# Modulation vectors by VectorE sums, an empty GpSimd, and due times in the planner of a two-layer diffusion backbone

## The chip, the cores and the metric

One core of a Trainium2 chip. The metric is the device time of one execution in microseconds, taken as the median of three runs. Engines are named as in the profile: PE (TensorE), DVE (VectorE), ACT (ScalarE), POOL (GpSimd), SP (SyncE, which issues the loads). PSUM is the memory that TensorE writes its products to, SBUF the other on-chip memory.

## The reference

Two layers work on 256 latent and 256 context tokens of 1024 features. Each has a SwiGLU FFN half step, a mixer, and a second FFN half step, all with a modulated RMS norm ahead:

```python
for l in range(DEPTH):
    mod_lat = jnp.split((silu_c @ w_mod[l] + b_mod[l])[:, None, :], N_MOD, axis=-1)
    mod_ctx = jnp.split((silu_cc @ w_mod[l] + b_mod[l])[None, None, :], N_MOD, axis=-1)
    x = macaron_half(x, mod_lat[0:3], norm_ffn1[l], w_ffn1_in[l], w_ffn1_out[l])
    ctx = macaron_half(ctx, mod_ctx[0:3], norm_ffn1[l], w_ffn1_in[l], w_ffn1_out[l])
    h_lat = modulate(rms_norm(x, norm_mix[l]), mod_lat[3], mod_lat[4])
    ...
    y_lat, y_ctx = hybrid_mixer(h_lat, h_ctx, w_in[l], ...)
    x = x + mod_lat[5] * (y_lat @ w_out[l])
    x = macaron_half(x, mod_lat[6:9], norm_ffn2[l], w_ffn2_in[l], w_ffn2_out[l])
    ...
return x
```

`macaron_half` is x + 0.5 * gate * swiglu(rms_norm(x) * (1 + scale) + shift); the FFN has 2816 hidden features. So each layer needs nine modulation vectors of 1024 features, for the latent condition c and for the context condition c_ctx, from a matrix w_mod of 1024 x 9216. The mixer runs two groups of heads on one input projection: eight heads of neighbourhood attention, and four heads of a DeltaNet in both directions. The DeltaNet's q, k and v pass a short convolution of five taps and a Silu, q and k are normalised and, for latent tokens, rotated (rope); chunks of 64 tokens need the inverse of I + A, with A the masked, decayed Gram matrix of the keys; the scans over the chunks carry a state. Both groups share an output projection. In layer 1 only the latent stream is finished.

## The kernel before

**Numbers and tiles.** Activations lie with features on partitions. Every dense product is split exactly into high and low parts in a rounded format (fp32r) and takes three products on TensorE (`mm3`). SP loads each weight tile of 128 x 1024 float32 (512 KB) into one of four buffers `wr`, ScalarE rounds it to `wh`, VectorE subtracts to `wl`. In the profile the products of an FFN read s (normed input) or d and n (hidden values), and wh or wl.

**Order.** The kernel isn't emitted as it is written. `Recorder` takes down every instruction with its data dependences; `plan` makes list schedules of all of them (`Schedule`) from a table of costs (`cost_of`) and the buffers that are free, at three widths of look-ahead, three times over, each in the order that the last one found; `emit` writes the best of them out, with products of zeros (`keep_warm`) where TensorE would idle. So all instructions have one line in the profile, L661 (L653 for the zeros, L680 and L672 after the change), and are told apart by the names of their tiles. An engine's next instruction is the ready one of lowest rank in the order before. All engines then run their own fixed queues.

**Modulation.** The first norm's two vectors come from `mods_first` by TensorE, from 32 half-size loads (n<-w_mod). The 16 others (`mods`; seven in the first FFN, four in the second FFN of layer 0, five in the first FFN of layer 1; twelve for two conditions, four for one) are sums on VectorE: the eight row tiles of w_mod's columns are scaled by the condition's value on each partition and added up, in pieces of 512 (or 1024) columns, in tiles `m`. `ps<-m,con` are the products with ones that add over the partitions; ScalarE copies the result, VectorE transposes it and adds the bias.

**The norm.** `norm_stats` and `norm_spread` make 1/rms of the tokens and spread it over partitions. `norm_apply` makes the normed, modulated input: for even feature tiles two VectorE operations (d<-x,na,d and s<-d,md,s) and one of ScalarE, for odd ones a GpSimd product (d<-x,d), two ScalarE operations and one of VectorE (s<-d,s). The running sums of squares are GpSimd's (`square_sum`).

**The DeltaNet.** `dn_qkv` makes q, k, v of a head from eight products in PSUM; ScalarE copies the sum (raw) and VectorE adds the four outer taps of the convolution (n<-n,sm,n of 508 and 510 elements, and half of that). `dn_prep` normalises (d<-ps,t) and, on GpSimd, rotates. `gate_math` is a chain of operations of 32 elements (gp, gs) on VectorE. `dn_unit` makes A for a token tile from decays and the keys' Gram matrix: its factors rg (n<-con,gh on VectorE and n<-con,gl on GpSimd) and B (d<-con,ex, d<-d,d, GpSimd). `dn_base` inverts blocks of 32, `dn_merge` merges them to 128; masks of the merge (wr<-d,con) are GpSimd's.

The GpSimd branch of the norm, as an example:

```python
nc.gpsimd.tensor_tensor(h, self.x[d][:, c], bs[:, :TL], O.mult)
nc.scalar.activation(h, h, self.A.Identity, bias=sh, scale=a[:, d, s:s + 1])
nc.scalar.copy(hh, h)
nc.vector.tensor_tensor(hl, h, hh.bitcast(F32), O.subtract)
```

Of the kernel before, what the change touches and what calls it, by code (L numbers as in the profile page):

```python
# [101 lines left out]
def lay_out(a):  # L102
# [11 lines left out]
        "xt": np.ascontiguousarray(xt.reshape(KD, 128, T).transpose(1, 0, 2)),  # L114
        "cc": np.stack([feat(a["c"][0]), feat(a["c_ctx"])], axis=-1),
# [19 lines left out]
class View:  # L135
    """A part of a planned tile: the cells it covers and how to reach it from the tile."""
# [39 lines left out]
def regroup(a, pat, kw):  # L176
    """numpy's view of an axis rearrangement in the notation of access patterns."""
# [31 lines left out]
class Sym:  # L209
    """A tile of the plan: a class of equal slots, and the slot that it is given."""  # L210
# [18 lines left out]
class Recorder:  # L229
    """Takes down the instructions of the kernel with their data dependences."""  # L230
# [9 lines left out]
    def tile(self, cls, bufs, shape, dtype, make, dram=False):  # L240
        """a new tile: the whole of it as a view."""
# [36 lines left out]
    def add(self, eng, ops):  # L278
# [3 lines left out]
        n.cost = sum(self.cost(eng, *o) for o in ops)  # L282
        n.columns = sum(columns_of(*o) for o in ops) if eng == "tensor" else 0
# [66 lines left out]

TABLES = {"Silu": "silu", "Exp": "exp", "Sqrt": "sqrt"}


class Pool:
    """A tile pool of the plan."""
# [26 lines left out]
class Clock:  # L382
    """The tensor engine's clock: half of its rate after a tick that counted few columns."""
# [6 lines left out]
    def run(self, t, cost, columns):  # L390
        """when work of so much time at the full rate and so many columns ends that begins at t."""
# [11 lines left out]
class Schedule:  # L403
    """Times for all nodes: a list schedule on the engines with the tiles' slots as a further resource."""

    def __init__(self, rec, rank, window, shift=None):
        self.rec, self.rank, self.window = rec, rank, window
        self.prio = [r - n.ahead for r, n in zip(rank, rec.nodes)]
        if shift:
            self.prio = [p + s for p, s in zip(self.prio, shift)]  # L410
# [3 lines left out]
    def prepare(self):  # L414
        """program order of the tiles in each class and how many are live where one begins."""
# [23 lines left out]
    def run(self):  # L439
# [22 lines left out]
        busy = {e: 0.0 for e in engs}  # L462
        table = None
# [12 lines left out]
        def foresee(i, at):  # L476
            """when urgent work can begin that is about to have all it waits for."""
# [7 lines left out]
        def claim(n):  # L485
            """slots for the tiles that begin with n, or the class that has none."""
# [43 lines left out]
        while done < len(nodes):  # L530
            # advance
# [19 lines left out]
            while again:  # L551
              again = False
              for e in engs:
                  held = []
                  while avail[e] and busy[e] <= t + 1e-9:
# [29 lines left out]
                      if e == "tensor":  # L585
# [3 lines left out]
                          en = clock.run(st, cost, n.columns)  # L589
                      else:  # L590
# [34 lines left out]
def keep_warm(rec, sched, cls):  # L625
    """matmuls of zeros into free PSUM slots where the tensor engine would stand idle."""
# [36 lines left out]

def plan(rec):
    """the best of a few schedules, each in the order that the one before it found."""
    n = len(rec.nodes)
    rank, best = list(range(n)), None
    for _ in range(3):
        found = min((Schedule(rec, rank, w).run() for w in (4, 12, 20)), key=lambda s: s.time)
        if best is None or found.time < best.time:  # L670
            best = found
        rank = [0] * n  # L672
        for k, i in enumerate(sorted(range(n), key=lambda i: (found.start[i], i))):
            rank[i] = k
    return best


def columns_of(name, a, kw):
# [3 lines left out]
    v = a[2]  # L682
# [1250 lines left out]
```

## Time and profile before

| | |
|---|---|
| median of three runs | 2002.95 us (2002.57 to 2003.49) |
| the profiled execution's own time | 2003.49 us |
| its span in the profile | 2003.5 us |
| stretches: start, first FFN | 0 to 42, 42 to 408 us |
| mixer of layer 0: units, merges | 450 to 550, 620 to 650 us |
| second FFN of layer 0, first of layer 1 | 776 to 1130, 1153 to 1515 us |
| mixer of layer 1: units, merges | 1560 to 1640, 1700 to 1730 us |
| second FFN of layer 1 | 1810 to 2004 us |

[...] Rows of operations give the tiles as out<-in, the count, the busy time and the mean of one in ns.

### The profile page before, as it was taken

The page shows a single profiled execution, that of the slowest core. Times are in us where ns is not written, and L with a number is a line of the kernel's source. Part 1 is how long each engine was busy: PE and PEld are TensorE (multiplying, and loading weights), DVE is VectorE, ACT ScalarE, POOL GpSimd, SP SyncE. Part 2 cuts the span into 40 slices and gives each one's busy share as a digit, 9 for nine tenths or more (in the row PEclk, how much of TensorE's full clock was granted, in tenths as well). Part 3 has the DMA queues.
Part 4 walks back from the last instruction along what each step waited for, and adds up shares of the span by engine and source line. Part 5 has one row for each costly group of instructions (what it writes and reads, how often), then busy time and mean ns, then how long its engine had stood idle before and what let it go on. Part 6 is the DMA issues. An engine that isn't in the chain of part 4 may idle for free.

```text
span 2003.5 us, 29224 instructions
## 1 busy us (share of the span) xinstructions
PE 1935.0 (97%) x11164; PEld 1621.5 (81%) x11164; DVE 1413.9 (71%) x2606; ACT 802.6 (40%) x1507; POOL 254.0 (13%) x257
## 2 busy tenths in 40 slices
PE   8999999998999999999999999999999789899999
PEld 5777777896787889777788888788888667699999
DVE  5777778879986979877333786553347999886555
ACT  4323222264546455332222433222126554755433
POOL 2000000036413003000000200000003641210000
PEclk8999999999998999999999999999999899899999
DMA  8556555541223223655233257653334133245653
GB/s 305 180 182 195 172 176 179 180 152 60 64 63 95 96 64 107 218 190 179 84 105 95 75 190 241 188 180 95 95 96 158 58 89 85 80 132 156 182 179 126
DMA packets 103611, 277.82 MB, mean 139 GB/s; under 512 B 26928, under 2 KB 30384, under 8 KB 103472
## 3 DMA queue, kind: packets, MB, share of 16 engines
q1 hardware_dynamic: 103472, 275.97, 43.9%
q8 instruction: 87, 1.43, 0.3%
q14 instruction: 52, 0.43, 0.1%
HBM read 267.54 MB, written 8.39 MB: 138 GB/s over the span
## 4 chain that ended last, share of the span: by engine, by line
PE 78%; DVE 16%; ACT 2%; issue 2%; DMA 1%; POOL 0%; SPq 0%; DVEq 0%; ACTq 0%; POOLq 0%
PE ps L661 78%; DVE n L661 3%; DVE d L661 3%; DVE t L661 2%; DVE wl L661 2%; DVE s L661 2%; DVE wh L661 1%; DVE x L661 1%; DVE gp L661 1%; DVE m L661 1%; ACT d L661 0%; ACT n L661 0%; ACT wh L661 0%; SPq L661 0%; ACT s L661 0%
## 5 line engine op out<-in xcount | busy, mean ns | idle before, releaser
L661 PE MATMUL ps<-s,wh 128*128 128x512 f32 (+2 forms) x3344 | 923.3, 364 | 6.6 <-ACT s L661 4.1
L661 PEld LDWEIGHTS ps<-s,wh 128*128 128x128 f32 (+1 forms) x3344 | 593.1, 190 | 116.4 <-issue 9.4
L661 PE MATMUL ps<-s,wl 128*128 128x512 f32 (+1 forms) x1672 | 606.1, 363 | 2.8 <-DVE wl L661 2.8
L661 ACT CAST wh<-wr 128x1024 fp32r<-128x1024 f32 (+2 forms) x341 | 350.0, 1037 | 612.5 <-PE ps L661 296.1
L661 DVE TENSOR_TENSOR wl<-wr,wh 128x1024 fp32r<-128x1024 f32 (+2 forms) x341 | 412.1, 1219 | 155.0 <-ACT wh L661 151.7
L661 PEld LDWEIGHTS ps<-s,wl 128*128 128x128 f32 x1672 | 317.3, 190 | 53.6 <-DVE wl L661 3.2
L661 PE MATMUL ps<-d,wh 128*128 128x256 f32 (+1 forms) x1344 | 297.5, 317 | 0.1
L661 DVE SCALAR_TENSOR_TENSOR m<-wr,sc,m 128x512 f32<-128x512 f32 (+1 forms) x364 | 267.2, 792 | 30.2 <-DMA wr<-w_mod 30.1
L661 PEld LDWEIGHTS ps<-d,wh 128*128 128x128 f32 x1344 | 220.3, 189 | 22.8 <-issue 3.0
L661 POOL TENSOR_TENSOR d<-d,d 128x256 f32<-128x256 f32 (+1 forms) x69 | 63.2, 916 | 1306.5 <-ACT d L661 1303.0
L661 DVE SCALAR_TENSOR_TENSOR x<-ps,hg,x 128x256 f32<-128x256 f32 x224 | 95.0, 477 | 174.4 <-PE ps L661 174.4
L661 PE MATMUL ps<-d,wl 128*128 128x256 f32 (+1 forms) x672 | 211.3, 314 | 0.0
L661 PE MATMUL ps<-n,wh 128*128 128x512 f32 (+1 forms) x640 | 179.2, 366 | 0.0
L661 PE MATMUL ps<-wh,s 128*128 128x512 f32 (+1 forms) x544 | 157.6, 364 | 0.2 <-ACT d L661 0.2
L661 ACT ACTIVATE d<-ps 128x512 f32<-128x512 f32 (+2 forms) x108 | 56.7, 530 | 209.2 <-PE ps L661 207.4
L661 DVE TENSOR_TENSOR d<-d,ps 128x512 f32<-128x512 f32 (+1 forms) x88 | 54.4, 619 | 113.5 <-PE ps L661 92.8
L661 PEld LDWEIGHTS ps<-d,wl 128*128 128x128 f32 x672 | 126.8, 189 | 8.5
L661 PEld LDWEIGHTS ps<-n,wh 128*128 128x128 f32 x640 | 114.8, 189 | 23.1 <-ACT wh L661 1.7
L661 PE MATMUL ps<-n,wl 128*128 128x512 f32 (+2 forms) x416 | 130.2, 347 | 0.0
L661 PEld LDWEIGHTS ps<-wh,s 128*128 128x128 f32 x544 | 97.3, 189 | 21.2 <-issue 5.6
L661 PE MATMUL ps<-wl,s 128*128 128x512 f32 (+1 forms) x272 | 97.6, 359 | 3.3 <-DVE wl L661 3.1
L661 DVE TENSOR_TENSOR d<-d,d 128x512 fp32r<-128x512 f32 (+29 forms) x248 | 83.6, 369 | 10.9 <-ACT d L661 6.8
(167 smaller groups left out, 1855.2 us busy)
## 6 DMA issues: line engine op xcount, KB each, us to landing
wr<-w_in SPq DMA_DIRECT2D x171, 512.0 KB, 4.1
wr<-w_mod SPq DMA_DIRECT2D x128, 512.0 KB, 3.7
wr<-w_out SPq DMA_DIRECT2D x104, 512.0 KB, 4.1
wr<-wd SPq DMA_DIRECT2D x24, 512.0 KB, 3.7
n<-w_mod SPq DMA_DIRECT2D x32, 256.0 KB, 5.4
wr<-wg SPq DMA_DIRECT2D x8, 528.0 KB, 3.5
xd<-x SPq DMA_DIRECT2D x16, 256.0 KB, 2.2
x<-xd SPq DMA_DIRECT2D x16, 256.0 KB, 2.7
```

What stands on the lines that cost most here:

```text
L661: getattr(eng, name)(*[rv(x) for x in a], **{q: rv(x) for q, x in k.items()})
```

## The change

**Modulation.** w_mod is packed with the 1024 rows of an output feature along the free dimension. `cond_rows` loads c and c_ctx, spread over all partitions, into two `m` tiles (512 KB each; three times in the program), and ScalarE takes their Silu. `mods` then makes one multiply-and-sum (`tensor_tensor_reduce`) for each tile of 128 output features and condition, which starts from the bias and leaves its sum in `md`; in the order it is two instructions of VectorE, printed ISA (junk and md, then md alone: the read of the accumulator). 224 such pairs take the place of 416 operations on VectorE, 64 products, 16 transposes, 16 additions and 16 ScalarE copies.

**GpSimd.** The norm's odd tiles go as the even ones, `bs` may stay in PSUM, sums of squares are VectorE's. Rope is VectorE's, from PSUM, and ScalarE scales by the norm afterwards, a tile at a time. rg's low part and B are scaled copies of ScalarE, four for each tile. The merge's masks are VectorE's, and a mask on A goes, as the last merge product is cut into halves (64 products of 64 x 64 instead of 32). The convolution reads PSUM without a copy. GpSimd has 36 instructions left of 262.

**Planner.** `due_times` gives every instruction the latest time by which it has to be done for TensorE's order; engines beside TensorE take the ready instruction that is due first. [...] Seven rounds instead of three, slightly other costs for products, 22 `d` buffers instead of 23.

```diff
 def pack_mod(w):
-    v = w.reshape(L, KD, 128, 9, 8, 4, 32)
-    return np.ascontiguousarray(v.transpose(0, 3, 1, 2, 5, 4, 6)).reshape(L, 9, KD, 128, 1024)
+    return np.ascontiguousarray(w.reshape(L, D, 9, KD, 128).transpose(0, 2, 3, 4, 1))
...
+        if due:
+            self.prio = [d if n.eng != "tensor" else p for p, d, n in zip(self.prio, due, rec.nodes)]
...
+                      elif n.port:
+                          en = port = max(st, port) + cost
...
+def due_times(rec, rank):
+    nodes, t, at = rec.nodes, 0.0, {}
+    for n in sorted((n for n in nodes if n.eng == "tensor"), key=lambda n: rank[n.i]):
+        t += n.cost
+        at[n.i] = t
+    due = [t + 50.0] * len(nodes)
+    for n in reversed(nodes):
+        due[n.i] = min([at.get(n.i, due[n.i])] + [due[j] - nodes[j].cost - LAT[n.eng][nodes[j].eng] for j in n.succs])
+    return due
...
-    for _ in range(3):
-        found = min((Schedule(rec, rank, w).run() for w in (4, 12, 20)), key=lambda s: s.time)
+    for _ in range(7):
+        found = min((Schedule(rec, rank, w, due).run() for w in (4, 12, 20)), key=lambda s: s.time)
...
+    def cond_rows(self):
+        nc = self.nc
+        self.cb = []
+        for n in range(2):
+            row = self.wp.tile([128, 1024], self.F32, name=self.nm("cb"), tag="m", bufs=self.BUFS["m"])
+            nc.sync.dma_start(row, self.io["cr"][:, n].to_broadcast([128, D]))
+            nc.scalar.activation(row, row, self.A.Silu)
+            self.cb.append(row)
+        yield
...
     def mods(self, l, lc, m, ns=2):
...
+        nc, O, md, cb = self.nc, self.O, lc["md"], self.cb
+        for d in range(KD):
             raw = self.wide("wr", "wr")
...
+            nc.sync.dma_start(raw[:, :D], self.io["w_mod"][l, m, d])
+            for n in range(ns):
+                c = 8 * m + d
+                nc.vector.tensor_tensor_reduce(self.junk, raw[:, :D], cb[n], 1.0, lc["bmod"][:, c:c + 1], O.mult, O.add, accum_out=md[:, c, n:n + 1])
+            yield
...
-            raw, acc = self.slot("cr", "n"), self.slot("ca", "n")
-            nc.scalar.copy(raw[:, :tok], ps[:, :tok])
+            acc = self.slot("ca", "n")
...
-            rv = raw[:, :tok].rearrange("p (s t) -> p s t", s=ns)
+            rv = ps[:, :tok].rearrange("p (s t) -> p s t", s=ns)
...
         for b in range(2):
-            nc.gpsimd.tensor_tensor(tv[:, :, b], ov[:, :, 1 - b], sn[:, :, b], O.mult)
-        nc.gpsimd.tensor_tensor(out[:, :TL], out[:, :TL], self.rope[:, 0], O.mult)
-        nc.gpsimd.tensor_tensor(out[:, :TL], out[:, :TL], tmp[:, :TL], O.add)
+            nc.vector.tensor_tensor(tv[:, :, b], pv[:, :, 1 - b], sn[:, :, b], O.mult)
+        nc.vector.tensor_tensor(out[:, :TL], ps[:, :TL], self.rope[:, 0], O.mult)
+        nc.vector.tensor_tensor(out[:, :TL], out[:, :TL], tmp, O.add)
+        for t, c in enumerate(tiles):
+            nc.scalar.activation(out[:, c], out[:, c] if t < 2 else ps[:, c], A.Copy, scale=rs[:, t:t + 1])
...
+            rg.append((d, self.slot("rg", "n", self.F32R)))
+            for h in range(4):
+                nc.scalar.activation(rg[-1][1][:, hc(h)], m, A.Copy, scale=self.gl.bitcast(F32)[:, t, 4 * d + h:4 * d + h + 1])
...
-            nc.gpsimd.tensor_tensor(self.h3(b), m3((self.lt, self.gt)[d]), b3(self.beta[:, t, 4 * d:4 * d + 4]), O.mult)
-        nc.gpsimd.tensor_tensor(B, B, B1, O.add)
+            for h in range(4):
+                nc.scalar.activation(b[:, hc(h)], (self.lt, self.gt)[d], A.Copy, scale=self.beta[:, t, 4 * d + h:4 * d + h + 1])
+        nc.vector.tensor_tensor(B, B, B1, O.add)
```

On VectorE in the first FFN, the sums of a vector (m, two conditions) stood between the low weight halves (wl) like this before:

```order
L661 SCALAR_TENSOR_TENSOR m_801<-wr_920,sc_81,m_801 128x2x256 x2
L661 SCALAR_TENSOR_TENSOR m_793<-wr_940,sc_81,m_793 128x2x256 x2
L661 SCALAR_TENSOR_TENSOR m_801<-wr_940,sc_81,m_801 128x2x256 x2
L661 TENSOR_TENSOR wl_1013<-wr_957,wh_984 128x1024
L661 TENSOR_TENSOR wl_1023<-wr_969,wh_996 128x1024
L661 SCALAR_TENSOR_TENSOR m_793<-wr_994,sc_81,m_793 128x2x256
L661 TENSOR_TENSOR d_1030<-d_1030,ps_953 128x512
L661 SCALAR_TENSOR_TENSOR m_793<-wr_994,sc_81,m_793 128x2x256
L661 SCALAR_TENSOR_TENSOR m_801<-wr_994,sc_81,m_801 128x2x256
L661 TENSOR_TENSOR n_1054<-d_1030,n_1045 128x512
```

and now, with md the vectors, junk a result that nothing reads, and m the two rows of conditions:

```order
L680 TENSOR_TENSOR wl_923<-wr_820,wh_916 128x1024
L680 ISA junk_803,md_400<-wr_884,m_657,sm_370 128x1024
L680 ISA md_400 128x1
L680 TENSOR_TENSOR d_948<-d_948,ps_874 128x512
L680 TENSOR_TENSOR wl_963<-wr_862,wh_955 128x1024
L680 TENSOR_TENSOR n_971<-d_948,n_961 128x512
L680 ISA junk_803,md_400<-wr_940,m_638,sm_370 128x1024
L680 ISA md_400 128x1
L680 ISA junk_803,md_400<-wr_940,m_657,sm_370 128x1024
L680 ISA md_400 128x1
L680 TENSOR_TENSOR wl_999<-wr_898,wh_994 128x1024
```

Two ISA pairs take the place of four operations of 512 elements, and the low halves stand between them as before.

On SP at the start, loads of the first modulation weights (n<-w_mod) alternated with half tiles of the first FFN weights (wr<-w_in):

```order
L661 DMA wr_201<-w_in 128x512
L661 DMA n_207<-w_mod 128x2x256
L661 DMA n_211<-w_mod 128x2x256
L661 DMA n_220<-w_mod 128x2x256
L661 DMA n_229<-w_mod 128x2x256
L661 DMA wr_242<-w_in 128x512
L661 DMA wr_253<-w_in 128x512
L661 DMA n_265<-w_mod 128x2x256
L661 DMA n_285<-w_mod 128x2x256
```

and now they come nearly in one piece:

```order
L680 DMA n_376<-w_mod 128x512
L680 DMA n_382<-w_mod 128x512
L680 DMA wr_388<-w_in 128x512
L680 DMA n_405<-w_mod 128x512
L680 DMA n_421<-w_mod 128x512
L680 DMA n_434<-w_mod 128x512
L680 DMA n_451<-w_mod 128x512
L680 DMA n_461<-w_mod 128x512
L680 DMA n_473<-w_mod 128x512
L680 DMA n_481<-w_mod 128x512
L680 DMA n_493<-w_mod 128x512
L680 DMA wr_510<-w_in 128x512
```

Of the half weights ten stood ahead of the last n<-w_mod load, and two do now; the 32 loads of n<-w_mod are the same.

On VectorE in the mixer of layer 0 there were no modulation sums. Now, between the convolution (n with sm, reading PSUM), rope (d<-ps,rope), the units' factors (n<-con,gh) and B's sum:

```order
L680 TENSOR_TENSOR d_4247<-ps_4224,rope_757 128x256
L680 TENSOR_TENSOR n_4252<-con_188,gh_3883 128x512
L680 TENSOR_TENSOR n_4259<-con_188,gh_3883 128x512
L680 TENSOR_TENSOR d_3848<-d_3848,d_3861 128x512
L680 ISA junk_803,md_400<-wr_3742,m_657,sm_370 128x1024
L680 ISA md_400 128x1
L680 ISA junk_803,md_400<-wr_3889,m_638,sm_370 128x1024
L680 ISA md_400 128x1
L680 SCALAR_TENSOR_TENSOR n_4291<-ps_4128,sm_370,n_4291 128x2x254
L680 ISA junk_803,md_400<-wr_3889,m_657,sm_370 128x1024
L680 ISA md_400 128x1
L680 SCALAR_TENSOR_TENSOR n_4291<-ps_4128,sm_370,n_4291 128x2x255
```

In all, 14 of the 224 pairs stand inside this mixer, 98 before it and 112 between the two mixers; none is in the mixer of layer 1. Counted in the same way, ScalarE's loads of function tables in the mixer of layer 0 go from 7 to 15 (31 to 39 in the program), and in the mixer of layer 1 some 45 more products with weights stand between the last `dn_unit` and the first `dn_merge` on TensorE.

## Rows read from the trace of the kernel before

**Rows 1.** the page, part 1: busy us, share of the span, instructions

```profile
PE 1935.0 (97%) x11164; PEld 1621.5 (81%) x11164; DVE 1413.9 (71%) x2606; ACT 802.6 (40%) x1507; POOL 254.0 (13%) x257
```

**Rows 2.** the page, part 4: shares of the chain that ended last

```profile
PE 78%; DVE 16%; ACT 2%; issue 2%; DMA 1%; POOL 0%; SPq 0%; DVEq 0%; ACTq 0%; POOLq 0%
```

**Rows 3.** windows: length, busy us (instructions) by engine, PEclk, DMA share, GB/s

```profile
0.00:42.00 42.00, 32.49 (x345) 22.60 (x345) 20.98 (x45) 19.52 (x48) 11.65 (x19) 0.88 0.92 321
42.00:408.00 366.00, 365.97 (x1717) 289.97 (x1717) 278.87 (x429) 106.94 (x143) 4.90 (x6) 1.00 0.56 178
450.00:550.00 100.00, 85.99 (x420) 69.30 (x418) 94.77 (x189) 52.61 (x128) 55.62 (x53) 0.95 0.21 65
620.00:650.00 30.00, 26.09 (x166) 19.52 (x165) 20.79 (x48) 24.50 (x85) 13.22 (x10) 0.77 0.38 114
1560.00:1640.00 80.00, 62.18 (x329) 51.39 (x329) 79.50 (x180) 41.29 (x99) 44.50 (x49) 0.91 0.24 71
1700.00:1730.00 30.00, 22.94 (x161) 14.26 (x160) 25.76 (x51) 24.53 (x76) 11.55 (x8) 0.77 0.36 85
```

**Rows 4.** timeline of DVE, gate arithmetic of layer 0: start, us, operation

```profile
451.62 1.23 DVE L661 TENSOR_TENSOR gp<-gp,gs 128x32 f32<-128x32 f32 x1
...
456.12 0.19 DVE L661 TENSOR_TENSOR gp<-gp,gs 128x32 f32<-128x32 f32 x1
```

**Rows 5.** timeline of POOL, the same stretch

```profile
448.51 3.04 POOL L661 TENSOR_TENSOR d<-con,ex 128x512 f32<-128x512 f32 x3 [18.77 <-ACT ge L661]
...
454.76 1.29 POOL L661 TENSOR_TENSOR d<-d,d 128x512 f32<-128x512 f32 x1
```

**Rows 6.** groups by line, PE: busy us, mean ns | idle before

```profile
L661 PE MATMUL ps<-m,con 128*32 128x512 f32 (+1 forms) x128 | 15.3, 551 | 0.0
```

**Rows 7.** groups by form, DVE, the whole program

```profile
L661 DVE SCALAR_TENSOR_TENSOR m<-wr,sc,m 128x512 f32<-128x512 f32 x336 | 231.3, 751 | 3.3 <-DMA wr<-w_mod 3.3
L661 DVE SCALAR_TENSOR_TENSOR x<-ps,hg,x 128x256 f32<-128x256 f32 x224 | 95.0, 477 | 174.4 <-PE ps L661 174.4
...
L661 DVE SCALAR_TENSOR_TENSOR m<-wr,sc,m 128x1024 f32<-128x1024 f32 x28 | 35.9, 1282 | 26.9 <-DMA wr<-w_mod 26.9
...
L661 DVE TENSOR_REDUCE mx<-ps 128x1 f32<-128x512 f32 x32 | 21.0, 678 | 0.1
...
L661 DVE TENSOR_TENSOR s<-d,s 128x256 fp32r<-128x256 f32 x44 | 19.8, 462 | 0.7 <-ACT s L661 0.6
...
L661 DVE SCALAR_TENSOR_TENSOR n<-ps,nec,d 128x128 f32<-128x128 f32 x48 | 13.6, 340 | 2.0 <-PE ps L661 1.9
```

**Rows 8.** groups by form, DVE, 42 to 408 us

```profile
L661 DVE SCALAR_TENSOR_TENSOR m<-wr,sc,m 128x512 f32<-128x512 f32 x196 | 133.2, 744 | 2.4 <-DMA wr<-w_mod 2.4
...
L661 DVE TENSOR_SCALAR m<-wr,sc 128x512 f32<-128x512 f32 x28 | 12.5, 473 | 1.0 <-PE ps L661 0.9
```

**Rows 9.** timeline of SP's queue at the start

```profile
32.30 6.61 SPq L661 DMA_DIRECT2D n<-w_mod  x8
```

**Rows 10.** groups by form, DVE, 1515 to 1660 us

```profile
L661 DVE SCALAR_TENSOR_TENSOR n<-n,sm,n 128x508 f32<-128x508 f32 x16 | 15.6, 976 | 0.8 <-ACT n L661 0.8
...
L661 DVE SCALAR_TENSOR_TENSOR d<-x,na,d 128x256 f32<-128x256 f32 x8 | 7.0, 922 | 1.6 <-ACT d L661 1.6
...
L661 DVE TENSOR_TENSOR gp<-gp,gs 128x32 f32<-128x32 f32 x7 | 3.9, 563 | 0.2
...
L661 DVE TENSOR_TENSOR d<-ps,t 128x512 f32<-128x512 f32 x4 | 2.7, 682 | 0.0
```

**Rows 11.** groups by form, ACT, the whole program

```profile
L661 ACT ACT_TABLE_LOAD x31 | 39.8, 1283 | 26.1 <-DVE n L661 20.5 <-DVE t L661 2.8 <-DMA ccraw<-cc 2.4
...
L661 ACT COPY n<-ps 128x512 f32<-128x512 f32 x50 | 29.3, 587 | 70.4 <-PE ps L661 69.9
...
L661 ACT ACTIVATE s<-d,ec 128x128 f32<-128x128 f32 x48 | 15.8, 394 | 1.2 <-PE ps L661 1.1
...
L661 ACT ACTIVATION_READ_ACCUMULATOR s<-ps,mx 128x1 f32 x48 | 9.7, 201 | 0.0
```

More of the change, by code (lines that the diff above doesn't have):

```diff
@@ L348, in __getattr__, with shares_port @@
         return lambda *a, **k: self._rec.op(self._name, op, a, k)
+def shares_port(eng, name, a, kw):
+    if name == "memset" or eng not in ("vector", "gpsimd"):
+        return False
+    if eng == "gpsimd":
+        return name != "dma_start"
+    size = lambda v: int(np.prod(v.shape[1:]))
+    out = a[0]
+    ins = [v for v in list(a[1:]) + [w for k, w in kw.items() if k != "accum_out"] if isinstance(v, View)]
+    ins = [v for v in ins if v.sym.cls[1] != "ps" and (size(v) > 1 or size(out) == 1)]
+    if name in ("tensor_tensor", "scalar_tensor_tensor", "tensor_tensor_reduce"):
+        return len(ins) > 1
+    return name in ("tensor_scalar", "tensor_copy") and len(ins) == 1 and out.sym.cls[1] != "ps"
 TABLES = {"Silu": "silu", "Exp": "exp", "Sqrt": "sqrt"}
@@ L908, in mods @@
-        ps, r = self.psum(), slice(0, 256 * ns)
-        with nc.bundle():
-            for j in range(4):
-                nc.tensor.matmul(ps[32 * j:32 * j + 32, r], self.ones[:, 0:32], acc[j // e][:, j % e].rearrange("p n c -> p (n c)"),
-                                 start=True, stop=True, tile_position=(0, 32 * j))
-        a, b = self.slot("ma"), self.slot("mb")
-        nc.scalar.copy(a[:, r], ps[:, r])
-        nc.vector.transpose(b[:, r], a[:, r])
-        v = b[:, r].rearrange("p (n d s) -> p d n s", n=ns, d=8)[:, :, :, 0]
@@ L1519, in dn_merge @@
         ec, lc = (v.rearrange("p (h c) -> p h c", h=4) for v in (xe[:, :256], xe[:, 256:]))
-        p2 = self.heads(lambda h: am[:, hc(h)], lambda h: ec[:, h], 64)
+        p2, lo, hi = self.psum(), slice(0, 64), slice(64, 128)
+        with nc.bundle():
+            for h in range(4):
+                for r, q in ((lo, hi), (hi, lo)):
+                    nc.tensor.matmul(p2[q, h * 64:h * 64 + 64], am[r, h * 128 + q.start:h * 128 + q.stop], ec[r, h], start=True, stop=True,
+                                     tile_position=(r.start, q.start))
         nc.vector.tensor_tensor(h4(y2, 2), bb(p2[:, :256].rearrange("p (h c) -> p h c", h=4), 2), mm(self.m64, 2), O.mult)
@@ L1862, in next_norm @@
             return after
-        bs = [self.norm_spread(self.norm_stats(s)) for s in range(2)]
+        bs = [self.norm_spread(self.norm_stats(s), True) for s in range(2)]
         self.norm_open()
@@ L1893, in program @@
             halves = (1, 0) if more else (0,)
-            self.fill += [self.mods(l, lc, m, 2 if more or m < 5 else 1) for m in range(4 if l else 2, 9)]
+            self.fill += [self.cond_rows()] + [self.mods(l, lc, m, 2 if more or m < 5 else 1) for m in range(4 if l else 2, 9)]
             a, b, c = f"a{l}" if l else "a", f"b{l}", f"c{l}"
@@ L1901, in program @@
                 lc2 = self.layer_consts(l + 1)
-                self.fill += [self.mods(l + 1, lc2, m) for m in range(4)]
+                self.fill += [self.cond_rows()] + [self.mods(l + 1, lc2, m) for m in range(4)]
                 nxt = next_norm(lc2, "1", 0, f"a{l + 1}")
```

78 lines of the change are left out of this document (29 added, 49 removed).

## Prediction

> **What bounds the kernel now.** I began with the busy times: TensorE is busy for 1935.0 of 2003.5 us, VectorE for 71%, ScalarE for 40% and GpSimd for 13% [rows 1]. But TensorE's busy time holds products of zeros that the program puts into idle places, so I took the chain of waits next: 78% of it is TensorE, 16% VectorE, and next to nothing is GpSimd or DMA [rows 2]. TensorE sets the pace, and VectorE does in some places. The windows tell where [rows 3]. From 42 to 408 us (the first FFN) TensorE is busy for 365.97 of 366.00 us at a granted clock of 1.00, and VectorE has 87 us free: what leaves TensorE there shortens the program, and work of VectorE is hidden. [...] The merges (620 to 650 and 1700 to 1730) have a clock of 0.77 and idle time on TensorE. At the start (0 to 42) the DMA share is 0.92, so loading sets it.
>
> Is that VectorE time real work? The timeline of the gate arithmetic says no [rows 4, 5]. An operation of 32 elements takes 1.23 us while GpSimd is in a run of operations of 512 elements, and the same operation 0.19 us when GpSimd has stopped. So VectorE pays for GpSimd's work, and in the two VectorE-bound stretches GpSimd is busy for 55.62 and 44.50 us [rows 3].
>
> **The sum** is made against the profiled execution, which took 2003.49 us with a span of 2003.5; it is the longest of the three, 0.5 us over their median, so nothing has to be converted.
>
> **Modulation products.** 64 fp32 products (ps<-m,con) leave TensorE, all in FFN stretches. They hold it for 15.3 us (the profile shows each as two) [rows 6], and TensorE is full there: -15.3.
>
> **Modulation sums on VectorE.** A tile with two conditions cost 4 x 0.751 = 3.0 us [rows 7]. Now it takes two multiply-and-sum instructions over 1024 elements, each followed by an accumulator read. The trace has no such pair. The nearest row for the first is the scalar_tensor_tensor of 1024 elements with two float32 sources in SBUF, 1.282 us [rows 7]; for the second, ScalarE's accumulator read, 0.201 us [rows 11]. A pair is 1.48 us and a tile 2.97: no change. The lower end is 1.28 (a free read), the upper is two passes, 2 x 1.282 + 0.201 = 2.77. I take 1.48, because multiply and add happen in one pass in the nearest row too. In the first FFN VectorE now has 278.87 us, of which 133.2 and 12.5 are the old sums [rows 3, 8]; the other 133 us and the 98 pairs that the new order has before the first mixer give 133 + 98 x 1.48 = 278 us, inside the 358 that TensorE needs without its 7 vectors' products: hidden, 0. The 16 transposes and ScalarE copies that go were hidden too.
>
> [...]
>
> **Start.** Ten half weights (0.26 MB each) stood between the loads of the first modulation weights; now two do, so the last of those, which go out until 38.9 us [rows 9], land 8 x 0.262 MB / 321 GB/s [rows 3] = 6.5 us earlier, and eight half weights land as much later. Either can decide: bounds -6.5 and +6.5. I take -4, since no feature tile can be multiplied before its modulation is there, while the products of the first tiles need two half weights only. The six new loads of the condition rows (512 KB each) go into FFN stretches with a DMA share of 0.56 [rows 3]: 0.
>
> **Layer 1, DeltaNet units (1560 to 1640).** At stake is 80 - 62.18 = 17.8 us of TensorE and 0.09 x 80 = 7 us of clock, 25 in all. What VectorE gets back when GpSimd is silent: at most GpSimd's 44.5 us; at least what single rows show [rows 10] against the same work undisturbed [rows 4, 7]: 16 conv operations at 976 against 751 ns, that is 3.6 us, and as much with those of 510 elements; 8 norm operations at 922 against 477, 3.6 us; 7 gate operations at 563 against 190, 2.6 us; with a few us of small operations that the rows don't give singly, some 16. I take 30, the middle, as in the timeline every small operation beside GpSimd lost all of the time above 0.2 us. What VectorE takes over: rope for 8 head tensors, each 2 x 0.340 + 0.477 + 0.462 = 1.62 us [rows 7], 13.0, less the scaling passes that go (4 x 0.682 and, half as long, 4 x 0.34 [rows 10], 4.1): 8.9; four B additions of about 0.6, 2.4; the norm's 8 odd tiles, two operations instead of one, 8 x 0.55 = 4.4. Together 16. VectorE is 30 - 16 = 14 us shorter and TensorE follows, as it is the one that waits; 2 of the 7 us of clock come with it: **-16**, bounds 0 and -25.
> The cover for what ScalarE takes over is its free time: 64 scaled copies of 128 elements at 0.394 = 25 us [rows 11], rope's scaling of 24 tiles at the same price 9, less 12 conv copies at 0.587 = 7 and some 5 of the norm: +22 on 41.29, 63 of the 64 us that the stretch would then have. That is tight; the second rival is made of it.
>
> **Layer 0, the same place (450 to 550).** At stake: 14.0 us and 0.05 x 100. Relief by the same share, 30/44.5 of 55.62, 37 us; taken over 16, and the new order has 14 multiply-and-sum pairs in this mixer, 14 x 1.48 = 21. Net **0**. With the low relief (16/44.5, 20 us) it is +17, with the high one -19. The due times put more ScalarE table loads here too (7 to 15 in the mixer), 8 x 1.283 = 10 us [rows 11], on 52.61 + 22 of 100: still covered, barely.
>
> **Merges.** Layer 1: idle 7.1 us and 0.23 x 30 = 6.9 of clock at stake. Some 45 more products of FFN and projection weights lie between the last unit and the first merge than before, and the masks that GpSimd made (11.55 us [rows 3]) cost VectorE 8 x 0.68 = 5.4. I take -5, bounds 0 and -14. Layer 0: 3.9 and 6.9 at stake; -4, bounds 0 and -11. The last merge product is cut into 64 of half height instead of 32: the nearest row is the modulation product, 15.3 / 64 = 0.24 us [rows 6], so 0 to 32 x 0.24 = +8; I take +1, as these have 64 columns instead of 512.
>
> 2003.5 - 15.3 - 4 - 16 + 0 - 5 - 4 + 1 = **1960 us**. The units, merges and start each miss by up to ten, so this case runs from 1942 to 1976.
>
> **Rivals.**
> *The mixers gain nothing.* ScalarE becomes the late one in the units (63 of 64 us above, with four-fold small copies ahead of every Gram product), so VectorE is freed only to wait for ScalarE. For it: the tightness above. Against it: ScalarE idles for half of these stretches now. Then 2003.5 - 15.3 - 4 + 1 = 1985.
> *Everything comes back.* The relief is near GpSimd's whole busy time; units -25 and -14, merges -10: 2003.5 - 15.3 - 4 - 25 - 14 - 10 + 1 = 1936. For it: the five- to six-fold durations in rows 4. Against it: the rest of VectorE's operations slow down far less.
> *No change.* Relief at the low end in both layers, so units 0 and +17, merges 0, the start as above: 2003.5 - 15.3 + 17 - 4 + 1 = 2002. For it: the undisturbed price of the conv operations stands in no row, only that of a like form. Against it: rows 4.
> *Slower: the multiply-and-sum takes two passes.* At 2.77 us a pair the first FFN has 133 + 98 x 2.77 = 404 us of VectorE in 358 of TensorE, and since its low weight halves stand in the same queue behind the pairs, TensorE waits: +46; the 14 pairs in the mixer add 14 x 1.29 = 18. 1960 + 64 = 2024. It decides from (358 - 133) / 98 = 2.3 us a pair. For it: a sum over the free dimension costs 678 ns for 512 elements [rows 7], a pass of its own length. Against it: ScalarE sums beside its main pass and reads the sum in 0.2 us.
>
> **How the numbers follow.** About 0.2%, 4 us, is what a measurement of this kernel can tell from no change. Forecast 0.57, mixers gain nothing 0.20, everything back 0.09, no change 0.05, two passes 0.09. The first three are faster: 0.86, with 0.05 the same and 0.09 slower. The range takes in forecast, the second rival and most of the gain above it: 1932 to 1994; outside lie no change, two passes and the thin tails, some 0.17.
>
> **What would show it.** Right: no ps<-m,con in the first FFN, and TensorE still at 99% or more there with VectorE at about 75%; a pair of 1.4 to 1.6 us; 32-element gate operations of 0.2 us throughout; VectorE's 508-element operations at 0.75 us; the units of layer 1 some 16 us shorter, those of layer 0 as long as before; GpSimd at 1% or less. Wrong: a pair above 2.3 us, with TensorE's idle time in the FFN put down to the low halves (wl); or VectorE idle in the units with ScalarE as the releaser; or conv operations that stay at 0.9 us with GpSimd silent, which would mean that they are slow by themselves and the relief is small.

## The result

The changed kernel takes 1953.41 us (median; 1951.56 to 1954.71) against 2003.18 beside it: a ratio of 0.9747, 95% interval 0.9734 to 0.976, 50 us faster. The forecast was 1960, the range 1932 to 1994. The profiled execution took 1952.2 us, its span is 1950.4, 53 below that of before.

The page of the change, part 1 (as [rows 1]), and part 4 (as [rows 2]):

```profile
PE 1901.5 (97%) x11145; PEld 1617.4 (83%) x11145; DVE 1366.0 (70%) x2776; ACT 833.3 (43%) x1612; POOL 26.9 (1%) x31
...
PE 76%; DVE 13%; ACT 4%; DMA 4%; issue 2%; SPq 0%; DVEq 0%; ACTq 0%
```

VectorE has 48 us less to do, although it and ScalarE (31 us more) took over nearly all that GpSimd did in 254 us. The windows of the change, at the places of [rows 3] (start, first FFN, the stretches that hold the units and the merges of layer 0, then of layer 1; they lie elsewhere now and differ in length); columns as there:

```profile
0.00:42.00 42.00, 34.52 (x441) 23.52 (x442) 22.95 (x64) 23.00 (x52) 5.54 (x11) 0.92 0.96 331
42.00:421.00 379.00, 369.86 (x1697) 306.29 (x1696) 269.11 (x416) 109.22 (x147) 1.31 (x4) 0.99 0.54 170
421.00:540.00 119.00, 116.41 (x666) 99.31 (x666) 112.06 (x296) 97.59 (x251) 3.19 (x2) 1.00 0.42 122
590.00:620.00 30.00, 26.64 (x185) 17.28 (x183) 23.18 (x53) 25.49 (x73) 9.00 (x6) 1.00 0.41 124
1528.00:1602.00 74.00, 68.08 (x387) 58.35 (x386) 69.62 (x204) 62.17 (x178) 3.53 (x2) 0.95 0.30 84
1645.00:1690.00 45.00, 39.62 (x328) 27.73 (x327) 35.87 (x87) 40.37 (x118) 2.71 (x2) 1.00 0.35 94
```

In the stretches with the units TensorE now works for 116 of 119 and 68 of 74 us (86 of 100 and 62 of 80 before, beside a VectorE that was busy for 94.77 and 79.50), and in the merges of layer 1 its granted clock (PEclk, a share of its full speed) went from 0.77 to 1.00. In layer 0 the low clock only moved behind the window, after 8 us in which TensorE was busy for 5.18:

```profile
612.00:620.00 8.00, 5.18 (x76) 3.16 (x76) 4.65 (x17) 7.68 (x25) 0.43 (x1) 1.00 0.44 142
620.00:628.00 8.00, 7.72 (x49) 7.08 (x49) 4.03 (x10) 5.48 (x21) 0.00 (x0) 0.52 0.57 177
628.00:636.00 8.00, 8.00 (x71) 7.38 (x64) 5.68 (x17) 5.75 (x11) 0.00 (x0) 0.84 0.01 2
```

That is 8 x 0.48 + 8 x 0.16 = 5 us of clock, of the 0.23 x 30 = 7 that were lost there before. And the first FFN, which was full before, has TensorE idle for 9 us. VectorE's groups by form (the first and the last are a modulation pair, the others answer to [rows 7, 10]):

```profile
L680 DVE CUSTOM_DVE_ANT_0 junk<-wr,m,sm 128x1024 bf16<-128x1024 f32 x224 | 287.6, 1284 | 235.0 <-DMA wr<-w_mod 231.9 <-DVE x L680 0.4
...
L680 DVE SCALAR_TENSOR_TENSOR d<-x,na,ps 128x256 f32<-128x256 f32 x72 | 31.9, 475 | 4.7 <-PE ps L680 4.4
L680 DVE SCALAR_TENSOR_TENSOR n<-ps,sm,n 128x508 f32<-128x508 f32 x40 | 29.6, 742 | 3.8 <-ACT n L680 3.7
...
L680 DVE DVE_READ_ACCUMULATOR2_ANT md<- 128x1 f32 x224 | 18.5, 83 | 0.0
```

The convolution's operations went from 976 ns in layer 1 to 742, the norm's from 922 to 475, and a pair takes 1.284 + 0.083 us. The timeline of the gate arithmetic in layer 0 has operations of 32 elements at 0.19 us throughout, where [rows 4] had 1.23:

```profile
449.83 0.19 DVE L680 TENSOR_TENSOR gp<-gp,gs 128x32 f32<-128x32 f32 x1
...
450.27 0.19 DVE L680 TENSOR_TENSOR gp<-gp,gs 128x32 f32<-128x32 f32 x1
```

To see where the 53 us came from, I cut both traces at the start of the last residual addition on VectorE in each part (x<-ps,hg,x for an FFN, x<-ps,md,x for a mixer); the last part goes on to the end of the span. The forecast column is the prediction's terms, the products' 15.3 us split by vectors (seven, four, five of 16).

| us | before | change | difference | forecast |
|---|---|---|---|---|
| start and first FFN, layer 0 | 419.1 | 421.2 | +2.1 | -10.7 |
| mixer, layer 0 | 352.7 | 336.1 | -16.6 | -3.5 |
| second FFN, layer 0 | 377.5 | 369.1 | -8.4 | -3.8 |
| first FFN, layer 1 | 376.4 | 373.6 | -2.8 | -4.8 |
| mixer, layer 1 | 275.8 | 250.9 | -24.9 | -20.5 |
| second FFN, layer 1 | 202.1 | 199.5 | -2.6 | 0 |

The forecast of 1960 is 7 us above the median (by the table, which is cut from one execution each, -43 stands against -53). But two rows are far off: the first FFN gave nothing, and the mixer of layer 0 gave what was expected of others.

### The profile page after: what moved, and what is told of

Its sections match the earlier page's. It is cut to its first block, busy times and chain, and to the rows that moved or that the text cites. A ratio compares the mean times of both kernels' runs of the same rounds, so it can differ in the third digit from the quotient of the medians.

```text
span 1950.4 us, 29083 instructions
## 1 busy us (share of the span) xinstructions
PE 1901.5 (97%) x11145; PEld 1617.4 (83%) x11145; DVE 1366.0 (70%) x2776; ACT 833.3 (43%) x1612; POOL 26.9 (1%) x31
## 4 chain that ended last, share of the span: by engine, by line
PE 76%; DVE 13%; ACT 4%; DMA 4%; issue 2%; SPq 0%; DVEq 0%; ACTq 0%
PE ps L680 76%; DVE d L680 3%; DVE n L680 2%; DMA wr<-w_mod 2%; DVE wl L680 2%; ACT d L680 1%; DVE wh L680 1%; ACT n L680 1%; DVE junk L680 1%; ACT wh L680 1%; DVE t L680 1%; DVE s L680 1%; DVE x L680 1%; ACT s L680 1%; ACT L680 1%
## 5 line engine op out<-in xcount | busy, mean ns | idle before, releaser
L680 PE MATMUL ps<-s,wh 128*128 128x512 f32 (+1 forms) x3344 | 912.9, 361 | 1.0 <-DVE s L680 0.5
L680 PEld LDWEIGHTS ps<-s,wh 128*128 128x128 f32 x3344 | 592.8, 189 | 100.3 <-issue 1.4
L680 DVE CUSTOM_DVE_ANT_0 junk<-wr,m,sm 128x1024 bf16<-128x1024 f32 x224 | 287.6, 1284 | 235.0 <-DMA wr<-w_mod 231.9
L680 DVE TENSOR_TENSOR d<-d,d 128x256 f32<-128x256 f32 (+29 forms) x310 | 111.6, 381 | 16.6 <-ACT d L680 12.0
L680 PEld LDWEIGHTS ps<-n,wl 128*128 128x128 f32 x416 | 71.9, 189 | 10.7 <-issue 0.8
```

The lines of the kernel that those rows point to most:

```text
L680: getattr(eng, name)(*[rv(x) for x in a], **{q: rv(x) for q, x in k.items()})
```

## The experiments

The first six take the change apart: modulation (M), GpSimd (G) and planner (P), each alone and in pairs. What P's diff calls a port is a rule of the plan: certain operations of VectorE and GpSimd are planned one after the other. Each has whole pieces of the diff above; the lines here only name them. M, G and P alone are edits of the kernel before (M brings its 22 buffers d along), the pairs are edits of the change. Ratios are to the kernel before, run beside each, and the differences follow from them; lengths of parts are from one profiled execution, cut as in the table.

**M alone.**

```diff
-                        nc.vector.scalar_tensor_tensor(o, w, c, o, O.mult, O.add)
+                nc.vector.tensor_tensor_reduce(self.junk, raw[:, :D], cb[n], 1.0, lc["bmod"][:, c:c + 1], O.mult, O.add, accum_out=md[:, c, n:n + 1])
```

> The kernel before with the modulation part of the change alone (weights packed the other way, multiply-and-sum pairs, no products with ones); GpSimd and the planner as before. Theory (the products stood on a saturated TensorE, each holding it for 1.1 to 1.2 us, the pairs are hidden): 64 products less, 2003 - 16 to 18 = 1986, the gain in the two to three FFN stretches only, TensorE at 99% there. Rival (the gain of the whole lies in the mixers and at the start, the products were half covered): 1995 or more.

1991.79 us, ratio 0.9942 (0.9928 to 0.9957), -12. By parts: first FFN 412.9, mixer 359.5, then 371.5 and 371.6: the FFNs gave 6.2 + 6.0 + 4.8 = 17 us, as by the theory, and the mixer of layer 0 took 6.8 back, with only 3 pairs in it; no run shows why.

**G alone.**

```diff
-            nc.gpsimd.tensor_tensor(h, self.x[d][:, c], bs[:, :TL], O.mult)
+        nc.vector.scalar_tensor_tensor(h, self.x[d][:, c], a[:, d, s:s + 1], bs[:, :TL], O.mult, O.mult)
```

> The kernel before with GpSimd's work moved away and nothing else. Theory (VectorE paid for GpSimd's work in the DeltaNet units; relief exceeds the work that it takes over): 2003 - 16 (units of layer 1) - 9 (merges) = 1978, with the conv operations of 508 elements at 0.74 us and the gate chain's at 0.2. Rival (what was gained in the mixers comes from the due times; emptying GpSimd only moves the load to ScalarE and VectorE): 1998 to 2010, with TensorE waiting for ScalarE in the units.

1970.91 us, ratio 0.9837 (0.9822 to 0.9852), -33. The theory, and more of it: mixers 335.8 and 265.1 us, so 17 in layer 0 and 11 in layer 1. The convolution's operations take 694 ns as a mean of their four forms (the same mean as in M and G, where those of 508 elements take 740), the gate chain's 0.19 us.

**P alone.**

```diff
+            self.prio = [d if n.eng != "tensor" else p for p, d, n in zip(self.prio, due, rec.nodes)]
```

> The kernel before with the planner's part alone: due times, the shared port, seven rounds, costs. Theory: it reorders the start (the first modulation weights first) and gains about 5 us there, and little in mixers that wait for VectorE's total work: 1996 to 2000. Rival (due times make the mixers' gain): 2003 - 5 - 25 = 1973. It could also be slower, as on a VectorE that is busy throughout a stretch any order has the same sum: 2003.

1998.67 us, ratio 0.9983 (0.9973 to 0.9993), -3: the theory. The 88th product with FFN weights starts at 54.1 us instead of 60.0; the mixers keep their length (356.4 and 275.0).

**M and G.**

```diff
-        found = min((Schedule(rec, rank, w, due).run() for w in (4, 12, 20)), key=lambda s: s.time)
+        found = min((Schedule(rec, rank, w).run() for w in (4, 12, 20)), key=lambda s: s.time)
```

> The change without the planner's part. Theory (parts add): 1986 + 1978 - 2003 = 1961, some 8 above the change. Rival (due times make the mixers' gain): 1985 or more. If it is at 1953 or lower, the planner's part gives nothing or costs.

1971.46 us, ratio 0.9838 (0.9821 to 0.9854): the modulation part gives nothing beside the emptied GpSimd, where it gave 12 alone. Neither expectation held well. By parts the first FFN has its gain (407.6), but the next two FFNs are longer than before (382.6 and 381.3). The trace shows where: ahead of each of them, TensorE multiplies zeros for 8.5 us while VectorE makes the norm. TensorE's timeline after the second FFN of layer 0 (left out between are the norm's own small products):

```profile
1128.00 1.59 PE L653 MATMUL ps<-zero 128*128 128x256 bf16 x13
...
1129.79 1.03 PE L653 MATMUL ps<-zero 128*128 128x256 bf16 x8
...
1131.59 5.84 PE L653 MATMUL ps<-zero 128*128 128x256 bf16 x52
```

VectorE's timeline at the same place, with a modulation pair in the queue ahead of the norm's reciprocal:

```profile
1129.11 1.28 DVE L661 CUSTOM_DVE_ANT_0 junk<-wr,m,sm 128x1024 bf16<-128x1024 f32 x1
1130.32 0.08 DVE L661 DVE_READ_ACCUMULATOR2_ANT md<- 128x1 f32 x1
1130.32 0.16 DVE L661 RECIPROCAL t<-t 128x2 f32<-128x2 f32 x1
```

The pair accounts for some 1.2 of the 8.5 us. G alone has 2.3 us of zeros at either place, as TensorE has other products (ps<-s,wh) ready there. So the rest lies in the order of the plan, and that the pairs brought that order about is not shown.

**M and P**, with GpSimd as before.

```diff
+            nc.gpsimd.tensor_tensor(self.h3(b), m3((self.lt, self.gt)[d]), b3(self.beta[:, t, 4 * d:4 * d + 4]), O.mult)
```

> The change without the emptied GpSimd. The parts alone gave -11 (modulation), -32 (GpSimd), -3 (planner); modulation and GpSimd together gave only -32, and all three -50, so some 17 come of the planner beside one of the others. Theory A (due times keep the multiply-and-sum pairs out of the way of the norms at the ends of the FFNs; in the run without the planner's part TensorE multiplied zeros there for 8 us twice): modulation and planner give more than their sum, 2003 - 11 - 3 - 8 = 1981 or less. Rival B (due times pay where VectorE and ScalarE took over GpSimd's work): 1988, the plain sum.

1980.75 us, ratio 0.9896 (0.9881 to 0.9911), -21: the number of theory A, but not its place. All FFNs have their gain (407.2, 372.3, 371.8), the mixers none (351.9, 275.8): without the emptied GpSimd there is no gain in them. But the two FFNs between are no shorter than in M alone (371.5, 371.6), where TensorE multiplies no zeros ahead of them; what the planner adds to M lies in the start and first FFN (412.9 to 407.2) and in the mixer of layer 0 (359.5 to 351.9). So the number was met, but not by the mechanism. The conv operations of 508 elements take 911 ns here (894 in the kernel before, all 40 of them).

**G and P**, with the modulation as before.

```diff
+                        nc.vector.scalar_tensor_tensor(o, w, c, o, O.mult, O.add)
```

> The change without its modulation part. Theory A: GpSimd and planner give their plain sum, 2003 - 32 - 3 = 1968, and the modulation part is worth 15 with the planner. Rival B: 1953 + 11 = 1964 at most, 1955 if the modulation part is worth nothing beside the others.

1948.96 us, ratio 0.9737 (0.9718 to 0.9756): rival B, and beyond it. GpSimd and planner alone are at least as good as the whole change. By parts against the change: first FFN 416.6 (421.2), mixers 335.3 and 243.3 (336.1 and 250.9), the FFNs between 375.1 and 379.2 (369.1 and 373.6). So the products' gain is there in the FFNs between, and lost in the first FFN and in the mixer of layer 1.

**The whole without due times.**

```diff
-        found = min((Schedule(rec, rank, w, due).run() for w in (4, 12, 20)), key=lambda s: s.time)
+        found = min((Schedule(rec, rank, w).run() for w in (4, 12, 20)), key=lambda s: s.time)
...
-        due = due_times(rec, rank)
```

> The whole change, with seven rounds, the shared port and the new costs, but without due times (every engine by the rank of the last order). If due times are what the planner's part is worth: as without that part, 1968 to 1973, with zeros on TensorE at the ends of the FFNs of layer 0 and 1. If the rounds and the costs are: 1953 to 1957.

1956.83 us, ratio 0.9777 (0.976 to 0.9794). Of the 18 us that the planner's part is worth beside M and G (1971.5 to 1953.4), due times are some 3; rounds, port and costs together are the rest. It is a mixed answer by place. The zeros stay (7.6 us ahead of each of the two FFNs between), and these FFNs take 382.7 and 380.5 us: there, due times are worth 20 us, and 5 more in the mixer of layer 1 (256.1). But the first FFN is at 406.0 us, so due times cost the change 15 there. They do so only beside the emptied GpSimd: M and P, which has them too, is at 407.2.

**Layer 0's ninth vector in the second FFN.**

```diff
-  ... for m in range(4 if l else 2, 9)]
+  ... for m in range(4 if l else 2, 9 if l else 8)]
-                self.fill += [self.cond_rows()] + [self.mods(l + 1, lc2, m) for m in range(4)]
+                self.fill += [self.cond_rows(), self.mods(l, lc, 8)] + [self.mods(l + 1, lc2, m) for m in range(4)]
```

> The change, with layer 0's ninth modulation vector (the gate of the second FFN) made at the start of that FFN instead of in the first, so that the filler's steps suffice and no pair is left for the mixer of layer 0 (counted in the order: 96 pairs in the first FFN, 80 in the second, none in the mixer). Theory (the 14 pairs, 19 us of a VectorE that is busy all through the units of layer 0, cost about half of that): 1953 - 9 = 1944, TensorE's products up to number 2500 some 9 us earlier. Rival (units of layer 0 have other cover, the pairs fill gaps): 1951 to 1955.

1952.5 us, ratio 0.9754 (0.9738 to 0.9769): no difference that can be told from the change. The mixer is 5 us shorter (330.9), the first FFN 3 longer (424.1). That pointed at the end of the first FFN, in the change's own trace. VectorE's timeline there:

```profile
380.94 1.28 DVE L680 CUSTOM_DVE_ANT_0 junk<-wr,m,sm 128x1024 bf16<-128x1024 f32 x1 [3.96 <-DMA wr<-w_mod]
382.15 0.08 DVE L680 DVE_READ_ACCUMULATOR2_ANT md<- 128x1 f32 x1
382.15 0.69 DVE L680 TENSOR_TENSOR d<-d,d 128x512 fp32r<-128x512 f32 x1
382.76 1.22 DVE L680 TENSOR_TENSOR wl<-wr,wh 128x1024 fp32r<-128x1024 f32 x1
```

and TensorE's, with its only two waits between 365 and 425 us:

```profile
385.30 0.77 PE L680 MATMUL ps<-d,wh 128*128 128x256 f32 x2 [3.86 <-DVE x L680]
...
404.04 0.61 PE L680 MATMUL ps<-con,d 128*128 128x1 f32 x4 [4.05 <-DVE d L680]
```

A pair stands at the head of VectorE's queue for 3.96 us until its weight tile has landed, and behind it wait the operations that read TensorE's results. The product at 385.30 was released by an addition (x<-ps,hg,x) that empties its PSUM bank. Twenty us later pairs stand between the norm's sums of squares (d<-d,d), and TensorE waits for those. These pairs waited for nothing; four of them, 5.3 us of VectorE, stand in the 17 us before the second wait ends. After the two waits the clock is 0.79 (384 to 392 us) and 0.83 (400 to 408), which costs another 3 us. Over the program VectorE's waits for w_mod tiles grew. The view of waits (us in total, times, longest), in the kernel before:

```profile
DVE m L661 <- DMA wr<-w_mod: 35.3, 23, 3.5
```

The same view of the change:

```profile
DVE junk L680 <- DMA wr<-w_mod: 231.9, 102, 5.2
```

The sum of these waits is not a price: without due times they come to 148.6 us, and the first FFN is the shortest of all. What counts is what stands behind such a pair.

**Pairs planned 2.5 us later after their load.**

```diff
-                          ready[j] = max(ready[j], en + LAT[e][m.eng])
+                          ready[j] = max(ready[j], en + LAT[e][m.eng] + (2.5 if m.ops[0][0] == "tensor_tensor_reduce" and e == "sync" else 0.0))
```

> The change, where the planner lets a multiply-and-sum start 2.5 us later after its load than other work (VectorE stood at the head of its queue for w_mod loads for 232 us in the change, 35 in the kernel before). Theory (at the end of the first FFN a pair that waits for its load holds up x<-ps, and TensorE idles 4 us for that): w_mod waits on VectorE below 120 us, 1953 - 4 to 9 = 1944 to 1949. Rival (the waits are hidden; a load buffer that is held longer delays weights): 1952 to 1960.

1934.83 us, ratio 0.9668 (0.9649 to 0.9687): 19 us below the change, twice what the theory expected. VectorE's waits for w_mod in the whole program:

```profile
DVE junk L681 <- DMA wr<-w_mod: 38.9, 28, 5.7
```

TensorE's only wait from 365 to 430 us:

```profile
PE ps L681 <- DVE d L681: 0.3, 1, 0.3
```

The first FFN takes 409.3 us (421.2 in the change), the mixer of layer 0 331.0 (336.1), the rest is unchanged to 0.3 us. Against the run without M (1948.96) the modulation part is now worth 14 us, nearly the products' 15.3.

**One more pass in each modulation sum.**

```diff
+    if name == "tensor_tensor" and "max" in str(a[3]):
+        return 0.001
...
+            for n in range(ns):
+                nc.vector.tensor_tensor(raw[:, :D], raw[:, :D], cb[n], O.max)
```

> The change with one more VectorE pass over each weight tile and condition (in place, its result is read by nothing; the planner counts it as nothing), so that a modulation sum costs 1.34 + 1.2 = 2.55 us, above the 2.3 from which the prediction's slower rival was to decide. Theory (VectorE then is over TensorE's time in the first FFN): 98 x 1.21 = 119 us on top of 269 of 379, +9 at least there, 14 x 1.2 = 17 in the mixer, and stalls by weight halves that come late: 1980 to 1995. Rival (the 232 us for which VectorE waits for w_mod loads take it up): 1953 to 1965.

2067.92 us, ratio 1.0338 (1.0316 to 1.0361): the theory's direction, three times its size. The first FFN took 486.8 us (+66), the second of layer 0 400.2 (+31). The windows of both (42 to 487, 830 to 1230 us):

```profile
42.00:487.00 445.00, 387.71 (x1711) 314.48 (x1711) 399.33 (x536) 109.32 (x148) 1.31 (x4) 0.94 0.46 148
830.00:1230.00 400.00, 376.50 (x1789) 312.09 (x1788) 303.40 (x420) 110.46 (x150) 0.00 (x0) 0.98 0.41 132
```

In the second, VectorE is busy for 303 of 400 us, and yet TensorE waited there 23.4 us for low weight halves (wl), in the first 35.3. A total that fits is no cover: the halves stand in the queue behind the sums. (The planner had not counted the pass, so its order was made for shorter sums, and the pass keeps each tile's buffer longer; these shares were not separated.)

**G and P with 22 buffers d.**

```diff
-    BUFS = {"s": 16, "n": 16, "d": 23, "x": 8, "m": 2, "wr": 4, "wh": 5, "wl": 5}
+    BUFS = {"s": 16, "n": 16, "d": 22, "x": 8, "m": 2, "wr": 4, "wh": 5, "wl": 5}
```

> The run without the modulation part (1949) with 22 buffers of the kind d instead of 23, as the change has. The change lost 8 us to it in the mixer of layer 1, where there are no pairs. If the buffer is the reason: 1953 to 1958, the mixer of layer 1 at 248 to 251 us. If not (the planner's luck with another list of work): 1947 to 1951, at 243.

1948.4 us, ratio 0.9741 (0.9726 to 0.9757), mixer of layer 1 at 242.8: the buffer isn't the reason for the 8 us there.

**Later pairs, and the ninth vector later.** The edits of the eighth and the ninth run together.

```diff
+                          ready[j] = max(ready[j], en + LAT[e][m.eng] + (2.5 if m.ops[0][0] == "tensor_tensor_reduce" and e == "sync" else 0.0))
...
+                self.fill += [self.cond_rows(), self.mods(l, lc, 8)] + [self.mods(l + 1, lc2, m) for m in range(4)]
```

> The last but two (a multiply-and-sum planned 2.5 us later after its load, 1935) together with layer 0's ninth vector made in the second FFN. In the 1935 run 16 pairs stand in the mixer of layer 0, here none. Theory (21 us of a VectorE that is busy all through the units cost about half): 1935 - 9 = 1926, all of it in the mixer of layer 0. Rival (pairs in the mixer fill gaps, as the first run of this edit without the later start suggested with 1952.5 against 1953.4): 1932 to 1937.

1932.79 us, ratio 0.9642 (0.9618 to 0.9666), not to be told from 1934.83. The rival: the mixer of layer 0 is 2.9 us shorter (328.1), not 9. By the trace six pairs still stand at its start (411 to 432 us), so ten pairs, 10 x 1.33 = 13 us of VectorE, cost 3 there. These two are the fastest kernels of the study, some 1% below the change.

## Why the prediction was right, and where it was not

**Modulation products, -15.3.** The size was right: alone the FFNs gave 17 us, and with pairs planned later after their loads the part is worth 14. In the change as it stands it is worth nothing (1953.4 with it, 1949.0 without). The step that failed is "hidden, 0" for the pairs in the first FFN. The sum of VectorE's work did fit, 269 of 379 us, as the prediction had it (278 of 358); but it was a sum. What it left out is that a pair is the first reader of its tile, and VectorE's queue is fixed: in the change's trace a load that landed late kept VectorE, and all that stood behind in its queue, waiting for 3.96 us. The prediction counted what an instruction costs and not what it may wait for, with TensorE's PSUM and the next norm behind it, nor that pairs which wait for nothing can stand ahead of a norm that TensorE needs. 12 of the forecast's 10.7 + 2.1 = 13 us in that stage came back with a later start for the pairs.

**Modulation sums, 1.48 a pair.** 1.284 + 0.083, and in a row one pair starts 1.33 us after the last (373.95 - 372.62 in the change's trace). The estimate was some 10% high, the choice of the one-pass row right. Another row of the kernel before has the form with one source:

```profile
L661 DVE TENSOR_SCALAR m<-wr,sc 128x1024 f32<-128x1024 f32 x4 | 3.0, 752 | 5.2 <-DMA wr<-w_mod 5.2
```

From 512 to 1024 elements it takes 279 ns more (473 [rows 8]), and the form with two sources 538 (744 [rows 8], 1282 [rows 7]): about half the throughput of the form with one source. The accumulator added nothing to that: 1284 ns with it. So the rival of two passes, at 2.77 us a pair, fell.

**Slower from 2.3 us a pair.** With the extra pass a sum took some 2.55 us, and the time rose by 115 us, where the prediction's way of counting gives 25 in the first FFN (133 + 98 x 2.55 = 383, against 358; 366 less 7/16 of 15.3 is 359, which changes little), 17 in the mixer and nothing in the second FFN. The sign was right, the price mis-sized, as the low halves stand in the queue behind the sums (35.3 and 23.4 us of waits).

**Start, -4.** The 300th product with FFN weights began 5.0 us earlier (104.3 for 109.3 us). The planner's part alone gives 6 there, GpSimd's alone 3.

**Layer 1, -16 and -5.** The mixer gave 24.9, for 21 forecast. That it comes of G is shown, not only argued: with GpSimd's work in its old place no run shortened the mixers by more than 3 us in layer 1 or 1 us in layer 0 (M, P, M and P), with it moved all did, by 10 to 33 and by 10 to 25. That the relief is contention is what the operations show: 976 to 742, 922 to 475, 1.23 to 0.19. The convolution and the norm changed an operand too, from SBUF to PSUM, so the trace of the kernel before has to decide: of its 40 convolution operations of 508 elements, the 20 that overlap no operation of GpSimd take 734 to 749 ns, as after the change, and the 20 that overlap one take 1049 as a mean and up to 1848. The operations of 32 elements, two inputs in SBUF, took about as long as GpSimd's own beside them (1.23 us beside 1.29 [rows 4, 5]). By what mechanism GpSimd's work holds up VectorE's, no run shows.

The same trace gives the size of the relief, which the sum had to guess. Taken against operations of the same form that overlap none of GpSimd's, the 275 that overlap one without reading PSUM lost some 98 us: 24 in the units of layer 0 and 23 in those of layer 1, where the sum took 37 and 30, and 39 and 44 in the whole mixers, of which the sum looked at the units and merges alone. The 53 that read an operand from PSUM lost nothing. So some of G's gain may come of the operands in PSUM and would be there beside a busy GpSimd; no run has them alone. Terms within the mixer (units, merges) were not tried singly.

**Layer 0, 0 and -4.** 16.6 came. Here the sum's 21 us for 14 pairs was too high a price: without M the mixer takes 335.8 and 335.3 us, with 14 pairs in it 336.1 and without them in the same change 330.9; with the later start 331.0 with 16 pairs and 328.1 with 6. So 10 to 14 pairs cost 3 to 5 us in a stretch that is full by the windows. With 4 in place of 21 the forecast's sum would give 17 + 4 = 21 us, somewhat more than came; with the measured relief of 24 in place of 37 as well, 8, so that the rest of the gain lies in parts of the mixer that the sum left out. The 4 us of the merges are in part not there: most of their clock is lost a little later.

**ScalarE, the second rival.** It came near: in the units of layer 1 ScalarE is busy for 62.17 of 74 us where I had reckoned 63 of 64, and TensorE's longest waits there are for it (5.1 us in four waits). It did not become the bound.

**The planner** was hardly priced at all beyond the start. Alone it gives 3 us; beside G it gives 22 (1970.9 to 1949.0), beside M and G 18. Due times are about 3 of those 18, net of the 15 that they lost in the first FFN; which of the seven rounds, the rule on the port and the costs gives the rest was not tried. Nor is it settled why the mixer of layer 1 takes 8 us less without the modulation part, although no pair stands in it; the number of d buffers is excluded, and with M and G alone the difference isn't there (264.3 and 265.1).

So the mechanism in the mixers was right in kind, and the closeness of the number was luck: two errors offset each other, 13 us too much hoped for in the first FFN and 13 too little in the mixer of layer 0.

## What to carry to other kernels

Work that is "hidden" in an engine with time to spare must also be asked what it waits for: in a queue of fixed order, an instruction that is the first to need a load holds up everything behind it (here once for 3.96 us, and TensorE with it for 3.86), and a few microseconds between load and reader in the plan were worth more here (19 us) than the products that the change removed. An idle-looking helper engine may be charged to another: compare the same operation beside the helper's work and away from it before counting its time as free, and look where its operands lie, as the 53 that read PSUM lost nothing here. And parts of a change to a planned kernel do not add: M, G and P alone sum to -48, G and P together give -53, and all three -50.

## What was not expected of the hardware

The accumulator read after a multiply-and-sum on VectorE takes 83 ns, against 201 for ScalarE's [rows 11], and the multiply-and-sum over 1024 float32 elements costs no more than a multiply-and-add of that size without a sum (1284 and 1282 ns). Beside GpSimd, VectorE's operations of 32 elements lost the most for their size, from 0.19 to 1.23 us. The 128x1024 subtractions (wl) seem to have lost nothing (1233 ns as a mean before, 1223 after), but only because most of them run in FFNs, where GpSimd was all but idle (4.90 of 366 us in the first [rows 3]): the 20 that overlapped its work took 1438 as a mean, the 303 that did not 1220. In the kernel before, VectorE has within 6 us three additions that read PSUM and one subtraction that doesn't:

```profile
1650.59 1.89 DVE L661 TENSOR_TENSOR x<-ps,d 128x512 f32<-128x512 f32 x3 [3.04 <-PE ps L661]
...
1654.83 2.31 DVE L661 TENSOR_TENSOR wl<-wr,wh 128x1024 fp32r<-128x1024 f32 x1
```

with GpSimd beside them in

```profile
1651.36 1.29 POOL L661 TENSOR_TENSOR wl<-x,con 128x512 f32<-128x512 f32 x1 [6.94 <-DVE x L661]
...
1654.32 1.73 POOL L661 TENSOR_TENSOR wl<-x,con 128x512 f32<-128x512 f32 x1
```

The last two additions overlap GpSimd's first operation and still take 0.68 us (they start 0.6 us apart); the subtraction takes 2.31 us instead of 1.22.
